# A decoder layer on one core: how the first loads are cut and queued, and the number of warm-up products

## The chip, the core and the metric

The kernel runs on one core of a Trainium2 chip. A core has five engines that run side by side and wait for one another on semaphores: TensorE (PE, matrix products into PSUM), VectorE (DVE), ScalarE (ACT), GpSimd (POOL) and SyncE (SP), which here only issues transfers. Transfers from HBM into SBUF (DMA) run on 16 DMA engines; an instruction on an engine's queue starts each of them. The metric is the device time of one execution in microseconds, the median over several runs.

## The reference

One layer of a hybrid decoder, 256 tokens, width 2048, all in float32:

```python
h = rms_norm(x, attn_norm_g[l])
proj = h @ w_in[l]                                   # 2048 x 4096
q, k, v, p = jnp.split(proj, [1024, 2048, 3072], axis=-1)
a = moba_attention(rms_norm(heads(q)), rms_norm(heads(k)), heads(v), rel_bias)   # 8 heads of 128
m = multiscale_pool(p, pool_w[l], pool_scale[l])     # causal windows 2, 4, 8, 16
x = x + jnp.concatenate([a, m], axis=-1) @ w_out[l]
x = x + conv_ffn(rms_norm(x, ffn_norm_g[l]), w_up[l], conv_w[l], conv_b[l], w_down[l])
```

(The norms' gains are left out in the line of `a`.) The feed-forward part has 2 x 5632 columns up, a causal depthwise convolution of width 3, a SiLU gate and a product down. Nearly all the time is the five matrix products with `w_in`, `pool_w`, `w_out`, `w_up` and `w_down`.

## The kernel before

**Tiling.** The host lays the weights out as chunks of 128 x 2048 floats (1 MB) in the order in which they are used; a chunk `c` holds two units, `u = 2c` and `2c + 1`, of 128 x 1024. A float32 product is made of three products of two-part numbers: each weight unit is split into `wh` (rounded, written by ScalarE, L111) and `wl` (the rest, by VectorE, L112), and each activation tile likewise into its two parts (`x_split`, L174 and L175, for the first product). TensorE multiplies `wh` with both parts and `wl` with the first.

**The first stage.** The program begins with the value columns of `w_in`, in steps of `tok_half` (L125 to L134). One step uses one unit: two k-tiles of 512 columns, and for each k-tile six products of 128 x 512 (four with `wh`, two with `wl`), all at L132. So unit 0 needs the k-tiles 0 and 1 of x and the first half of chunk 0, unit 2 the k-tiles 4 and 5 of x and the first half of chunk 1, and so on; eight units make a block.

**The order of work.** There is no planner: the order of instructions on each engine is the order in which this program writes them. Before the first step it writes all first loads, then `x_split(k)` and `split_piece` for the eight k-tiles 0 to 7, alternating, 512 columns at a time, so that ScalarE makes xh 0, wh 0, xh 1, wh 1, ... and VectorE the rests in the same order. Unit 4 is split next, as a whole. Then step `u` splits unit `u + 5` (`AHEAD`) and multiplies unit `u`.

**The loads.** Raw chunks live in four buffers (`RAWS`). `load(c, pieces, j)` (L98) transfers piece `j` of `pieces` of a chunk, `load_xT(k0, k1)` (L166) the k-tiles `k0` to `k1` of the transposed x, a k-tile being 128 x 256 floats (128 KB; the first has 8 KB more with the norm's gains). x and the chunks 0 to 3 make 2 + 4 MB and are the first loads. When a chunk is split, `release` (L119) starts the load of the chunk four further on, on SyncE's queue, where it waits for the VectorE instruction that last read the buffer. Transfers of SyncE and ScalarE take eight completion semaphores in turn: in the listing of the program the ninth transfer waits on its queue until the first has landed, the tenth until the second has, and so on.

**The warm-up.** While the first loads are under way TensorE multiplies a tile of ones with itself (L184), into a PSUM tile that nothing reads.

Of the kernel before, what the change touches and what calls it, by code (L numbers as in the profile page):

```python
# [69 lines left out]
def layer(ctx: ExitStack, tc: tile.TileContext, xT, wts, par, relT, ident_d, onehot_d, icnt_d, out):  # L70
    nc = tc.nc
# [15 lines left out]
    def small(name):  # L87
        return sm.tile([P, 512], F32, name=name, tag="small")
# [6 lines left out]

    raws, wparts = {}, {}

    def load(c, pieces=1, j=0, queue=None):  # L98

        if c not in raws:  # L100
            raws[c] = wpool.tile([P, CH], F32, name="raw", tag="raw", bufs=RAWS)
        s = slice(j * CH // pieces, (j + 1) * CH // pieces)
        (queue or nc.sync).dma_start(raws[c][:, s], wts[c][:, s])

    def split_piece(u, lo, n):
        r, o = raws[u // 2], (u % 2) * HALF
# [12 lines left out]
    def release(c):  # L119

        raws.pop(c)
        if c + RAWS < wts.shape[0]:
            load(c + RAWS)
# [42 lines left out]
    def load_xT(k0, k1):  # L166

        c = slice(KT + k0 * S if k0 else 0, KT + k1 * S)
        nc.sync.dma_start(xboth[:, c], xT[:, c])
# [8 lines left out]


    nc.vector.memset(ones, 1.0)  # L180
    load(0, 4, 0, nc.scalar)
    ps = small("ps_start")
    for _ in range(7):
        nc.tensor.matmul(ps[:, :P], ones, ones, start=True, stop=True)  # L184
    nc.scalar.preload_act_table_set("natural_log_exp_and_others")

    for k in range(4):
        load_xT(k, k + 1)
        if k:
            load(0, 4, k)  # L190
    for u in range(2, 8):
        load_xT(2 * u, 2 * u + 2)
        load(u // 2, 2, u % 2)
    for k in range(8):
        x_split(k, k + 1)
        split_piece(k // 2, (k % 2) * 512, 512)
# [276 lines left out]
    for b in range(2):  # L473
# [4 lines left out]
        for j in range(4):  # L478
            h, u = 4 * b + j, at + 2 * j
# [198 lines left out]
```

## Time and profile before

| | us |
|---|---|
| median of 3 runs | 1048.32 (1047.69 to 1049.33) |
| profiled execution | 1049.49 |
| its span, first instruction to last | 1047.70 |
| TensorE busy | 1039.4 |
| VectorE busy | 715.8 |
| ScalarE busy | 537.4 |

The profiled execution is one run of the program with the hardware profiler; its own time is a little longer than its span. In the views, L111 is line 111 of the kernel; "out<-in" names the tiles an instruction writes and reads; "[1.14 <-ACT wh L111]" says that the engine stood idle for 1.14 us and what ended the idle time. An engine's queue is marked with a q (SPq, ACTq): these rows are instructions that issue a transfer. Matrix products are pipelined, so a row's busy time overlaps that of the next; the pace of TensorE is read from the starts.

### The profile page before, as it was taken

To read this page: it belongs to the slowest core of one execution; us is meant where nothing else is said; L and a number is where in the kernel's file an instruction comes from. 1 tells how busy PE (TensorE), PEld (TensorE's weight loads), DVE (VectorE), ACT (ScalarE), POOL (GpSimd) and SP (SyncE) were. 2 spreads that over 40 slices of the span, in tenths; PEclk is the share of its full clock that TensorE was granted. 3 is DMA by queue.
4 is the path that set the end of the run, shared out by engine and by line. 5 is a ranking of instruction groups with operands and counts; after the bars stand their busy time and mean duration, and the time that the engine had idled before them with its cause. 6 is when DMAs were issued, how large, how long until landed. Compare 5 with 4: busy or idle time off the path is not lost.

```text
span 1047.7 us, 14301 instructions
## 1 busy us (share of the span) xinstructions
PE 1039.4 (99%) x5784; PEld 898.9 (86%) x5784; DVE 715.8 (68%) x906; ACT 537.4 (51%) x709; POOL 54.8 (5%) x44
## 2 busy tenths in 40 slices
PE   9999999999999999999999999999999999999998
PEld 7878788888888888888888888888888888888887
DVE  6845657776667777777555677777765567777762
ACT  7644544555645555565444455555544445555541
POOL 0500003600110000000000000000000000000000
PEclk9999999999999999999999999999999999999999
DMA  9777554556454445445555445455465545445541
GB/s 348 264 213 226 186 181 141 181 218 225 163 202 176 184 173 220 171 165 219 206 188 188 161 170 220 174 186 216 161 224 179 199 154 210 161 182 219 211 152 41
DMA packets 31395, 200.47 MB, mean 191 GB/s; under 512 B 3816, under 2 KB 4872, under 8 KB 8544
## 3 DMA queue, kind: packets, MB, share of 16 engines
q1 hardware_dynamic: 30192, 196.66, 51.1%
q0 software_dynamic: 992, 2.63, 1.5%
q8 instruction: 45, 0.74, 0.3%
q10 hardware_dynamic: 144, 0.26, 0.1%
q14 instruction: 22, 0.18, 0.1%
HBM read 195.86 MB, written 3.67 MB: 190 GB/s over the span
## 4 chain that ended last, share of the span: by engine, by line
PE 94%; DMA 2%; DVE 2%; POOL 1%; ACT 1%; issue 0%; ACTq 0%; DVEq 0%; POOLq 0%
PE ps_feat L139 54%; PE ps_feat L141 27%; PE ps_tok L132 10%; DMA raw<-in_wts 2%; PE ps_feat L148 1%; DVE wl L112 1%; PE ps_pool L148 1%; PE ps_s L321 1%; POOL pa L380 0%; DMA xboth<-in_xT 0%; ACT wh L111 0%; PE ps_T L308 0%; PE ps_av L353 0%; PE ps_eT L343 0%; DVE m L292 0%
## 5 line engine op out<-in xcount | busy, mean ns | idle before, releaser
L112 DVE TENSOR_TENSOR wl<-raw,wh 128x1024 fp32r<-128x1024 f32 (+1 forms) x366 | 445.0, 1251 | 180.8 <-ACT wh L111 180.1
L139 PE MATMUL ps_feat<-x2h,wh 128*128 128x512 f32 x1408 | 493.2, 393 | 0.0
L111 ACT ACTIVATE wh<-raw 128x1024 fp32r<-128x1024 f32 (+1 forms) x366 | 368.8, 1041 | 136.0 <-PE ps_feat L139 96.5
L141 PE MATMUL ps_feat<-x2h,wl 128*128 128x256 f32 x1408 | 392.8, 279 | 0.0
L139 PEld LDWEIGHTS ps_feat<-x2h,wh 128*128 128x128 f32 x1408 | 263.8, 187 | 62.9
L141 PEld LDWEIGHTS ps_feat<-x2h,wl 128*128 128x128 f32 x1408 | 263.8, 187 | 0.0
L139 PE MATMUL ps_feat<-hid,wh 128*128 128x512 f32 x680 | 238.1, 393 | 0.0
L141 PE MATMUL ps_feat<-hid,wl 128*128 128x256 f32 x680 | 189.7, 279 | 0.0
L139 PEld LDWEIGHTS ps_feat<-hid,wh 128*128 128x128 f32 x680 | 127.4, 187 | 30.3
L141 PEld LDWEIGHTS ps_feat<-hid,wl 128*128 128x128 f32 x680 | 127.4, 187 | 0.0
L369 ACT ACTIVATE fs<-ps_feat 128x512 f32<-128x512 f32 x75 | 44.9, 599 | 129.9 <-PE ps_feat L141 129.9
L132 PE MATMUL ps_tok<-wh,xh 128*128 128x512 f32 x384 | 108.3, 404 | 1.1 <-ACT wh L111 1.1
L370 DVE TENSOR_TENSOR fs<-ps_feat,fs 128x512 f32<-128x512 f32 x75 | 51.9, 692 | 63.9 <-ACT fs L369 63.9
L139 PE MATMUL ps_feat<-cat,wh 128*128 128x512 f32 x256 | 89.7, 393 | 0.0
L132 PEld LDWEIGHTS ps_tok<-wh,xh 128*128 128x128 f32 x384 | 72.4, 191 | 18.7 <-ACT wh L111 1.4
L556 ACT ACTIVATE y<-u,pv 128x256 f32<-128x256 f32 x88 | 48.2, 595 | 65.8 <-DVE u L551 65.8
L141 PE MATMUL ps_feat<-cat,wl 128*128 128x256 f32 x256 | 71.4, 279 | 0.0
L557 DVE SCALAR_TENSOR_TENSOR y<-u,pv,y 128x256 f32<-128x256 f32 x88 | 42.3, 481 | 29.7 <-ACT y L556 29.7
L132 PE MATMUL ps_tok<-wl,xh 128*128 128x512 f32 x192 | 60.9, 399 | 0.0
L139 PEld LDWEIGHTS ps_feat<-cat,wh 128*128 128x128 f32 x256 | 48.0, 187 | 11.3
L141 PEld LDWEIGHTS ps_feat<-cat,wl 128*128 128x128 f32 x256 | 48.0, 187 | 0.0
L139 PE MATMUL ps_feat<-xh,wh 128*128 128x512 f32 x128 | 46.6, 404 | 0.0
(112 smaller groups left out, 555.6 us busy)
## 6 DMA issues: line engine op xcount, KB each, us to landing
raw<-in_wts SPq DMA_DIRECT2D x177, 1024.0 KB, 4.9
raw<-in_wts SPq DMA_DIRECT2D x6, 512.0 KB, 7.8
x<-in_xT SPq DMA_DIRECT2D x1, 2048.0 KB, 9.3
out<-x SPq DMA_DIRECT2D x7, 256.0 KB, 2.0
xboth<-in_xT SPq DMA_DIRECT2D x6, 256.0 KB, 7.6
band<-rsb POOLq DMA_DIRECT2D x1, 1536.0 KB, 37.3
T<-band POOLq DMA_DIRECT2D x2, 512.0 KB, 7.5
raw<-in_wts SPq DMA_DIRECT2D x3, 256.0 KB, 4.1
```

The lines of the kernel that those rows point to most:

```text
L111: nc.scalar.activation(wh, w, AF.Copy)
L112: nc.vector.tensor_tensor(wl, w, wh.bitcast(F32), op=OP.subtract)
L132: nc.tensor.matmul(ps[:, t, :], act[:, k0 + k, a, t * P:(t + 1) * P], w[:, ws], start=(first and k == 0 and n == 0), stop=(last and k == 1 ...
L139: nc.tensor.matmul(ps, wh[:, ws], act[:, k, :, :], start=(first and n == 0), stop=False, skip_group_check=True)
L141: nc.tensor.matmul(ps[:, S:], wl[:, ws], act[:, k, 0, :], start=False, stop=(last and n == len(ks) - 1), skip_group_check=True)
L148: nc.tensor.matmul(ps, w[:, ws], act[:, k, a, :], start=(first and n == 0 and i == 0), stop=(last and n == len(ks) - 1 and i == 2))
L321: nc.tensor.matmul(ps[:, s], qT[:, j, t * P:(t + 1) * P], kT[:, j, :(t + 1) * P], start=(t == 0), stop=True, skip_group_check=True)
L369: nc.scalar.activation(dst, ps[:, :, S:], AF.Copy)
L370: nc.vector.tensor_tensor(dst, ps[:, :, :S], dst, op=OP.add)
L556: nc.scalar.activation(y[:, m, :], u[:, m, 2:], AF.Identity, scale=cw[2], bias=col(C_CB + f))
L557: nc.vector.scalar_tensor_tensor(y[:, m, :], u[:, m, 1:1 + S], cw[1], y[:, m, :], op0=OP.mult, op1=OP.add)
```

## The change

The first piece of chunk 0 is no longer issued from ScalarE's queue. All first loads stand in SyncE's queue, x and weights by turns: k-tile 0 and 1 of x each with a quarter of chunk 0, then k-tiles 2 and 3 with the second half of chunk 0, then four k-tiles with a whole chunk, three times. There were 20 first loads, 19 of them on SyncE, and there are 12. Nine warm-up products stand where seven stood. The splits, the products and all later loads are written in the same order as before.

```diff
-    def load(c, pieces=1, j=0, queue=None):
+    def load(c, pieces=1, j=0):
...
-        (queue or nc.sync).dma_start(raws[c][:, s], wts[c][:, s])
+        nc.sync.dma_start(raws[c][:, s], wts[c][:, s])
...
     nc.vector.memset(ones, 1.0)
-    load(0, 4, 0, nc.scalar)
     ps = small("ps_start")
-    for _ in range(7):
+    for _ in range(9):
         nc.tensor.matmul(ps[:, :P], ones, ones, start=True, stop=True)
     nc.scalar.preload_act_table_set("natural_log_exp_and_others")
 
-    for k in range(4):
-        load_xT(k, k + 1)
-        if k:
-            load(0, 4, k)
-    for u in range(2, 8):
-        load_xT(2 * u, 2 * u + 2)
-        load(u // 2, 2, u % 2)
+    for k0, k1 in ((0, 1), (1, 2), (2, 4)):
+        load_xT(k0, k1)
+        load(0, 4 // (k1 - k0), k0 // (k1 - k0))
+    for c in range(1, 4):
+        load_xT(4 * c, 4 * c + 4)
+        load(c)
     for k in range(8):
         x_split(k, k + 1)
         split_piece(k // 2, (k % 2) * 512, 512)
```

## The prediction

> **What bounds the kernel now.** I read the busy table first, then the chain of waits for the first 45 us, the timeline of the first 14 us, and the DMA issues of that stretch with their times to landing.
>
> ```profile
> PE 1039.4 (99%) x5784; PEld 898.9 (86%) x5784; DVE 715.8 (68%) x906; ACT 537.4 (51%) x709; POOL 54.8 (5%) x44
> ...
> PEclk9999999999999999999999999999999999999999
> ```
>
> TensorE is busy for all but 8.3 of 1047.7 us. The chain of the first 45 us (start, length, what):
>
> ```profile
> 0.74 3.71 DMA xboth<-in_xT
> 4.47 0.51 ACT xh L174
> 4.98 0.53 ACT wh L111
> 5.55 38.26 PE ps_tok L132 x156
> ```
>
> The end hangs on the first x piece, ScalarE's two copies (xh, wh) and the first product at 5.55; from there TensorE never waits until 43.81. A change of the first loads can therefore act only by moving products before about 20 us. Such a shift then reaches the end whole, because the later loads are tied to the splits, not to the clock (SP's waits over the whole run: us, times, longest):
>
> ```profile
> SPq L103 <- DVE wl L112: 897.2, 175, 10.5
> ```
>
> The timeline, merged (start, length, engine; "x4" counts instructions):
>
> ```profile
> 0.74 0.41 ACTq L103 DMA_DIRECT2D raw<-in_wts  x1
> 0.74 0.86 SPq L169 DMA_DIRECT2D xboth<-in_xT  x2
> 1.06 3.35 PE L184 MATMUL ps_start<-ones 128*128 128x128 f32 x14 [1.06 <-DVE ones L180]
> 1.65 0.42 SPq L103 DMA_DIRECT2D raw<-in_wts  x1
> 3.58 0.43 SPq L103 DMA_DIRECT2D raw<-in_wts  x1
> 4.89 0.61 ACT L111 ACTIVATE wh<-raw 128x512 fp32r<-128x512 f32 x1
> 5.03 0.43 SPq L103 DMA_DIRECT2D raw<-in_wts  x1
> 5.55 2.08 PE L132 MATMUL ps_tok<-wh,xh 128*128 128x512 f32 x4 [1.14 <-ACT wh L111]
> 5.99 0.43 SPq L103 DMA_DIRECT2D raw<-in_wts  x1
> 8.28 1.33 PE L132 MATMUL ps_tok<-wh,xh 128*128 128x512 f32 x4
> 9.91 1.10 PE L132 MATMUL ps_tok<-wh,xh 128*128 128x512 f32 x4
> 11.19 0.63 ACT L111 ACTIVATE wh<-raw 128x512 fp32r<-128x512 f32 x1 [2.26 <-DMA raw<-in_wts]
> 11.32 1.10 PE L132 MATMUL ps_tok<-wh,xh 128*128 128x512 f32 x4
> 12.13 0.62 ACT L111 ACTIVATE wh<-raw 128x512 fp32r<-128x512 f32 x1
> 12.73 1.10 PE L132 MATMUL ps_tok<-wh,xh 128*128 128x512 f32 x4
> 13.14 1.05 SPq L103 DMA_DIRECT2D raw<-in_wts  x2
> 13.86 0.69 DVE L112 TENSOR_TENSOR wl<-raw,wh 128x512 fp32r<-128x512 f32 x1
> ```
>
> A k-tile is six products. From 9.91 to 11.32 and on to 12.73 it takes 1.41 us; the first took 2.73 (5.55 to 8.28) and the second 1.63. So 1.32 + 0.22 = 1.54 us were lost to slow first products, though the granted clock in the page's slices reads 90% or more from the first on. The second thing to see is 11.19: ScalarE had idled 2.26 us for the first half of chunk 1, and that wh was ready at 11.82, only 0.91 us ahead of the product at 12.73 that reads it. This is the nearest miss in the stretch.
>
> **The loads.** Issues with KB and us to landing, asked for the stretches around 1.65, 3.58, 5.03, 5.99 and 13.14 us:
>
> ```profile
> raw<-in_wts SPq DMA_DIRECT2D x1, 256.0 KB, 4.0
> raw<-in_wts SPq DMA_DIRECT2D x1, 256.0 KB, 4.2
> raw<-in_wts SPq DMA_DIRECT2D x1, 512.0 KB, 6.1
> raw<-in_wts SPq DMA_DIRECT2D x1, 512.0 KB, 7.1
> raw<-in_wts SPq DMA_DIRECT2D x1, 512.0 KB, 7.8
> ```
>
> Counting the pieces issued up to each, 1544 KB (136 + 3*128 + 4*256) had landed at 3.58+4.2 = 7.8 us; 2312 KB at 11.1; 3080 KB, which ends chunk 1, at 5.99+7.1 = 13.1; 6152 KB, which ends chunk 3, at 13.14+7.8 = 20.9. The engines were never short of work; they were slow in one stretch (busy times, then granted clock, DMA share, GB/s):
>
> ```profile
> 8.00:12.50 4.50, 4.50 (x20) 3.59 (x19) 2.25 (x6) 2.23 (x5) 0.00 (x0) 1.00 0.98 320
> 13.00:18.00 5.00, 5.00 (x23) 4.04 (x22) 4.85 (x9) 5.00 (x10) 0.00 (x0) 1.00 1.04 413
> ```
>
> **The change, part by part.**
>
> *Chunk 0's first piece goes from ACT's queue to the second place of SP's.* ACT is rid of a 0.41 us issue, worth nothing: its next wait is for x at 4.47. The weights are issued at about 1.2 instead of 0.74 (two SP issues took 0.86). With the 4.0 us of the piece issued at 1.65 they land at 5.2, wh takes 0.61, and the first product starts near 5.85: +0.3. The lower bound is 0, since x alone held ScalarE to 4.47 and SP's queue now has less beside it. I take +0.3.
>
> *Two more warm-up products.* Seven end at 4.41, so one is 3.35/7 = 0.48 us, and nine end near 5.4, ahead of 5.85: they delay nothing. What they can bring is at most the 1.54 us, if TensorE is at full rate from its first product. Then unit 2 (chunk 1's first half) is wanted at 5.85 + 4*1.41 = 11.5; without it, at 13.0. Both ends stay open, and the next part decides whether they matter.
>
> *Fewer, larger pieces: 20 loads become 12.* SP issues seven fewer (7*0.43 = 3 us of its queue) and is past all of them by about 6.5 us. Chunks 4 and 5, next in that queue, go out earlier but stand behind the first loads, so they gain and cost nothing. Chunk 0's second half is now one piece; 1544 KB still end it, so by the row above it lands near 7.8, its wh is ready at 8.4, and TensorE wants it at 5.85 + 2.82 = 8.7: covered by 0.3 us. Chunk 1 is the part without cover. It was two halves with x between, wh waiting for 2312 KB; it is now a single 1024 KB piece behind four x tiles, and ScalarE's wait for it ends only when 3080 KB have landed. The trace of before bounds that: 13.1, when the same bytes had landed, from above; from below, 7.8 plus 1536 KB at the steady rate of (6152-3080)/(20.9-13.1) = 394 KB/us = 3.9 us, so 11.7. I take 12.7, an estimate near the upper end: 13.1 is the row of the same bytes in the same stretch, and the slowness there (320 against 413 GB/s) has no cause that the trace names, so most of it is kept; 0.4 us of the 1.4 between the ends is credited to fewer and longer transfers. wh then takes 0.62 and TensorE about 0.04, so unit 2 starts at 13.4 instead of 12.73: **+0.65 us**. The warm-up's gain and the first product's loss both lie in front of this wait and are swallowed by it: unit 2 is wanted at 11.5 to 13.0 in either case. Were the cover gone (an early chunk 1), they would be worth -1.54 and +0.3.
>
> *Behind it.* In the trace of before ScalarE went on from one k-tile's wh to the next in 0.94 us (11.19, 12.13) against 1.41 on TensorE, so each later wh gains about 0.47 us; DVE runs a step behind (the row at 13.86 is the wl of unit 3's first k-tile, which TensorE reaches at 12.73 + 2.82 = 15.55). Chunk 2 ends at 4616 KB, by the steady rate at 13.1 + 3.9 = 17.0, chunk 3 at 20.9; units 4 and 6, their first readers on TensorE, come at 13.4 + 5.64 = 19.0 and 24.7. No second wait.
>
> *Sum.* Profiled execution: 1049.49 us, 1.79 outside the span. It stands 1.17 above the median of 1048.32. Part of that is the slow first products: unit 2 cannot start before the 11.82 of its wh, 0.91 earlier than profiled, and I give the fastest run (1047.69) that start; the other 1.80 - 0.91 = 0.89 I put down to profiling. So 1049.49 + 0.65 - 0.89 = **1049.25 us**, +0.9 on the median. The new kernel should also scatter less, since the wait for chunk 1 no longer depends on how fast the first products run.
>
> The Trainium skill's page "DMA: Bandwidth & Descriptors", section "Anatomy of one DMA", fits a transfer as about 2.0 us plus its bytes at 436 GB/s. As an estimate by that page, 3080 KB from 0.74 would have landed near 10.0, and chunk 1 would make TensorE wait for nothing. The trace does not agree: those bytes had landed at 13.1.
>
> **The rivals.**
>
> *B, chunk 1 arrives in time (faster side).* If the slow stretch of 8 to 12.5 us does not come back, it lands at 11.7, unit 2 starts at 12.37, and the time is 1049.25 - 1.03 = 1048.2. For it: from 13 us on the same queue moved 413 GB/s. Against it: nothing in the change touches the cause, as far as one is to be seen. Earlier still, with TensorE at full rate, 11.5 is the floor: 1047.35. To be faster by more than 0.2% (2.1 us, about what a measurement of this kernel can tell from no change, so under 1046.2) about 1.1 us of the 1.79 outside the span would have to go with ACT's unused queue too; no row shows such a cost. Call that D.
>
> *C, chunk 1 arrives as late as the next whole chunks do (slower).* The first two 1024 KB pieces, issued at 13.86 and 15.57:
>
> ```profile
> raw<-in_wts SPq DMA_DIRECT2D x1, 1024.0 KB, 9.5
> raw<-in_wts SPq DMA_DIRECT2D x1, 1024.0 KB, 11.0
> 15.57 0.33 SPq L103 DMA_DIRECT2D raw<-in_wts  x1
> ```
>
> Issued near 4.0, chunk 1 would by these land at 13.5 to 15.0; the middle, 14.25, gives unit 2 at 14.9 and 1050.75. From a landing of about 13.9 on it is slower by more than 0.2%. Against it: the first of them had up to 4096 KB to wait for, itself included (7176 less the 3080 landed at 13.1), chunk 1 has 3080.
>
> *G, the wait slows TensorE again (slower).* If the full rate comes early, TensorE stands from 11.5 to 13.4, 1.9 us, longer than any pause after its start. If that costs the slow rate once more, the price is again about 1.54 us: 1050.8. No row of before shows such a pause.
>
> The page "TensorE: Matmul & The Clock Gate" of the Trainium skill, Part 1, has the array at half clock until a window of some 3.4 us, running freely, was busy, and back there after about as long an idle one. The doubled first k-tile (2.73 against 1.41) agrees with its first half; by its second, 1.9 us would not suffice, and G would be empty.
>
> That the nine products change nothing of the rate is no separate case: the forecast does not need them.
>
> **How the numbers follow.** Forecast 0.48 (its own range 1048.8 to 1050.1, landing 12.2 to 13.5), B 0.18, C 0.18, G 0.10, D 0.06. The range runs from B to the middle of C and a little past: 1047.8 to 1051.2, leaving out D and the later half of C. Slower by over 0.2% (above 1050.4): C, G and 0.02 of the forecast, 0.30. Faster: D, 0.06. Within: 0.64.
>
> **What would show it.** In the new profile: ScalarE's wait before the first wh of chunk 1 ends at 12 to 13.5 us and TensorE has a gap there of 0.4 to 2 us (right), or no gap (B), or one past 14 (C); first k-tile at 1.4 instead of 2.73 us shows the warm-up worked; k-tiles of over 2 us after the gap show G. If the first product starts after 6.5 us, the first step was mis-sized; if a gap stands at chunk 0's second half or at chunk 2, the cover that I claim there was wrong.

## The result and the profile after

The changed kernel takes 1050.77 us (median of 15 runs, 1050.05 to 1051.83); the kernel before, over 15 runs, 1049.18 (1047.69 to 1050.01). The ratio is 1.0015, with an interval of 1.0008 to 1.0021: about 1.6 us slower, inside the 0.2% that the prediction took as its bound, though the interval just reaches past it. The profiled execution of the changed kernel took 1050.82 us, its span 1049.0. The busy table says as little as before:

```profile
PE 1040.2 (99%) x5788; PEld 899.0 (86%) x5788; DVE 715.9 (68%) x906; ACT 537.7 (51%) x709; POOL 54.6 (5%) x44
```

TensorE's busy time has grown by 0.8 us, about what the two added products take (4.21 us for nine, 3.35 for seven), and its idle time by 0.5. Where the time went is read from the chain of waits of the first 45 us (start, length, what):

```profile
2.59 0.43 SPq L169
...
3.06 0.43 SPq L103
...
3.54 0.43 SPq L169
...
4.01 9.55 DMA raw<-in_wts
...
13.58 0.64 ACT wh L111
...
14.26 30.95 PE ps_tok L132 x131
```

The chain no longer runs over x and the first product at 5.55. It runs through SyncE's queue (rows like the first three, back to 0.74) to the issue of chunk 1 at 4.01, waits 9.55 us for it to land, and only then goes on over ScalarE to unit 2 on TensorE at 14.26. The timeline of the changed kernel, cut to the rows that answer to those of before:

```profile
1.06 4.21 PE L183 MATMUL ps_start<-ones 128*128 128x128 f32 x18 [1.06 <-DVE ones L180]
...
2.91 0.51 ACT L174 ACTIVATE xh<-xboth 128x256 fp32r<-128x256 f32 x1 [0.90 <-DMA xboth<-in_xT]
...
4.62 0.63 ACT L111 ACTIVATE wh<-raw 128x512 fp32r<-128x512 f32 x1 [1.20 <-DMA raw<-in_wts]
...
5.30 2.02 PE L132 MATMUL ps_tok<-wh,xh 128*128 128x512 f32 x4
...
7.62 1.10 PE L132 MATMUL ps_tok<-wh,xh 128*128 128x512 f32 x4
...
9.08 0.63 ACT L111 ACTIVATE wh<-raw 128x512 fp32r<-128x512 f32 x1 [1.22 <-DMA raw<-in_wts]
...
9.77 1.20 PE L132 MATMUL ps_tok<-wh,xh 128*128 128x512 f32 x4 [0.58 <-ACT wh L111]
...
13.58 0.63 ACT L111 ACTIVATE wh<-raw 128x512 fp32r<-128x512 f32 x1 [2.15 <-DMA raw<-in_wts]
...
14.26 1.20 PE L132 MATMUL ps_tok<-wh,xh 128*128 128x512 f32 x4 [1.42 <-ACT wh L111]
...
15.77 1.10 PE L132 MATMUL ps_tok<-wh,xh 128*128 128x512 f32 x4
```

Four things changed on the way to unit 2. The first product starts at 5.30 instead of 5.55 (-0.25). The first two k-tiles end at 7.62 + 1.41 = 9.03, so they lost 0.91 us to slow products instead of 1.54 (-0.63). Unit 1 waits from 9.03 to 9.77 for chunk 0's second half (+0.74). Unit 2 could start at 9.77 + 2.82 = 12.59 and starts at 14.26 (+1.67). The sum is +1.53, which is 14.26 - 12.73. The two whole executions differ by 1.33, because some 0.2 us come back later: a wait of TensorE for the query heads (ps_T) is 0.3 us in place of 0.7.

The rate of the DMA engines in three stretches (busy times, then granted clock, DMA share, GB/s), first before, then after:

```profile
4.50:8.00 3.50, 2.45 (x6) 1.99 (x7) 2.95 (x6) 3.45 (x8) 0.00 (x0) 1.00 1.05 377
8.00:12.50 4.50, 4.50 (x20) 3.59 (x19) 2.25 (x6) 2.23 (x5) 0.00 (x0) 1.00 0.98 320
12.50:18.00 5.50, 5.50 (x25) 4.45 (x24) 5.35 (x11) 5.50 (x11) 0.00 (x0) 1.00 1.03 408
```

```profile
4.50:8.00 3.50, 3.47 (x12) 2.67 (x12) 1.86 (x4) 2.17 (x4) 0.00 (x0) 1.00 0.91 274
8.00:12.50 4.50, 3.92 (x18) 2.79 (x16) 2.56 (x5) 2.06 (x4) 0.00 (x0) 1.00 1.01 395
12.50:18.00 5.50, 4.08 (x18) 3.06 (x17) 3.76 (x8) 4.42 (x10) 0.00 (x0) 1.00 1.03 429
```

The slow stretch did not stay at 8 to 12.5 us; it moved to 4.5 to 8. Over both stretches together the engines moved nearly the same: 377 x 3.5 + 320 x 4.5 = 2760 thousand bytes before, 274 x 3.5 + 395 x 4.5 = 2737 thousand after.

### The profile page after: what moved, and what is told of

It is laid out like the page before. It is cut to its first block, busy times and chain, and to the rows that moved or that the text cites. A ratio compares the mean times of both kernels' runs of the same rounds, so it can differ in the third digit from the quotient of the medians.

```text
span 1049.0 us, 14294 instructions
## 1 busy us (share of the span) xinstructions
PE 1040.2 (99%) x5788; PEld 899.0 (86%) x5788; DVE 715.9 (68%) x906; ACT 537.7 (51%) x709; POOL 54.6 (5%) x44
## 3 DMA queue, kind: packets, MB, share of 16 engines
HBM read 195.86 MB, written 3.67 MB: 190 GB/s over the span
## 4 chain that ended last, share of the span: by engine, by line
PE 94%; DMA 2%; DVE 2%; POOL 1%; ACT 1%; issue 0%; SPq 0%; ACTq 0%; DVEq 0%; POOLq 0%
PE ps_feat L139 54%; PE ps_feat L141 27%; PE ps_tok L132 10%; DMA raw<-in_wts 2%; PE ps_feat L148 1%; DVE wl L112 1%; PE ps_pool L148 1%; PE ps_s L319 0%; POOL pa L378 0%; ACT wh L111 0%; PE ps_T L306 0%; PE ps_av L351 0%; PE ps_eT L341 0%; DVE m L290 0%; POOL pst L380 0%
```

## The experiments

Theory W, from the prediction: a product waits for all bytes up to the end of its piece, the wait for chunk 1 sets the time, and what happens ahead of it is swallowed. Its rivals are given with each run. Times are medians; each kernel ran beside the kernel before. Starts and landings are read from the one profiled execution of each kernel.

**Seven products again.**

```diff
 # the changed kernel
-    for _ in range(9):
+    for _ in range(7):
```

> The changed kernel with seven warm-up products again, nothing else. Theory W (the wait for the whole chunk 1 swallows what the warm-up does): unit 2 still starts at 14.0 to 14.5 us, because the wait for chunk 1 ends at about 13.5; the median stays within 0.3 us of the changed kernel's 1050.77. Rival (the two products carry a gain of their own that reaches the end): slow first products cost up to 0.6 us more, and the median is 0.6 to 1.3 us above, 1051.4 to 1052.1.

Measured: 1051.01 us (1050.22 to 1051.81), 0.24 above the changed kernel. In its profile:

```profile
5.25 2.08 PE L132 MATMUL ps_tok<-wh,xh 128*128 128x512 f32 x4 [0.84 <-ACT wh L111]
...
7.98 1.53 PE L132 MATMUL ps_tok<-wh,xh 128*128 128x512 f32 x4
...
10.56 1.20 PE L132 MATMUL ps_tok<-wh,xh 128*128 128x512 f32 x4 [0.58 <-ACT wh L111]
...
14.33 1.19 PE L132 MATMUL ps_tok<-wh,xh 128*128 128x512 f32 x4 [0.70 <-ACT wh L111]
```

The first k-tile takes 2.73 us again and unit 1 is 0.79 us later (10.56 against 9.77), yet unit 2 is only 0.07 later. The wait in front of unit 2 swallowed the difference, as theory W has it.

**Nine products with the old loads.**

```diff
 # the kernel before
-    for _ in range(7):
+    for _ in range(9):
```

> The kernel before with nine warm-up products, loads as they were. Theory W: with the old loads nothing waits behind the first products until about 11.8 us, so a faster start reaches the end: median 0.3 to 1.2 us under the kernel before (1049.18 over 15 runs), 1048.0 to 1048.9, and the slow runs near 1049.9 become rare. Rival (the two products do nothing for the rate): 1049.0 to 1049.4 with the same scatter. The second look at the old loads also shows whether the slow stretch of the DMA engines from 8 to 12.5 us comes back at the same place: if it belongs to these loads, about 320 GB/s there again; if it is chance, elsewhere or nowhere.

Measured: 1048.43 us (ten runs 1047.98 to 1049.06, one 1050.21), 0.75 under the 1049.18 of the runs beside it, but a ratio of 0.9998 with an interval of 0.9989 to 1.0006, which alone settles nothing (the quarters below do). The profile shows the mechanism: the first k-tile takes 1.50 us (5.38 to 6.88) and unit 2 starts at 11.61, after a wait of 0.35 us.

```profile
5.38 1.20 PE L132 MATMUL ps_tok<-wh,xh 128*128 128x512 f32 x4
...
6.88 1.10 PE L132 MATMUL ps_tok<-wh,xh 128*128 128x512 f32 x4
...
11.61 1.20 PE L132 MATMUL ps_tok<-wh,xh 128*128 128x512 f32 x4 [0.35 <-ACT wh L111]
```

The slow stretch is at its old place, 317 GB/s from 8 to 12.5 us and 366 from 4.5 to 8, so with the same loads it came back once.

**Chunk 1 in halves again.**

```diff
 # the changed kernel
-    for c in range(1, 4):
+    for u in range(2, 4):
+        load_xT(2 * u, 2 * u + 2)
+        load(u // 2, 2, u % 2)
+    for c in range(2, 4):
         load_xT(4 * c, 4 * c + 4)
         load(c)
```

> The changed kernel with chunk 1 in two halves again and the k-tiles 4 to 7 of x in two pairs, ordered as before; chunks 2 and 3 whole, first piece on SyncE's queue, nine products. Theory W (a product waits for all bytes up to the end of its piece): the first half of chunk 1 now ends at 2312 KB instead of 3080, at about 13.5 - 768/390 = 11.6 us, unit 2 starts at 12.6 where the products before it end, and the median falls by 1.3 to 1.7 us to 1049.1 to 1049.5. Rival (the loads as a whole are slow in the new order, and the size of chunk 1's piece does not matter): unit 2 stays near 14.2 and the median within 0.3 us of 1050.77.

Measured: 1049.70 us, 1.07 under the changed kernel; ten of its eleven runs are faster than the fastest of the changed kernel's fifteen (1050.05). Unit 2 starts at 12.45, 1.81 us earlier than in the changed kernel, which is theory W. That the time fell by less has a reason the theory left out. TensorE now reaches unit 4 at 18.08, while chunk 2, still one piece, is not split:

```profile
17.61 0.63 PE L132 MATMUL ps_tok<-wl,xh 128*128 128x512 f32 x2
18.34 1.20 PE L132 MATMUL ps_tok<-wh,xh 128*128 128x512 f32 x4
19.60 0.73 PE L132 MATMUL ps_tok<-wl,xh 128*128 128x512 f32 x2
20.17 1.10 PE L132 MATMUL ps_tok<-wh,xh 128*128 128x512 f32 x4
```

Unit 4 starts 0.26 us late and its first k-tile takes 1.83 instead of 1.41 us, because the wl of a whole unit follows its wh: 0.7 us in all.

**The first piece on ScalarE's queue again.**

```diff
 # the changed kernel, load() with its queue argument as before the change
+    load(0, 4, 0, nc.scalar)
...
-        load(0, 4 // (k1 - k0), k0 // (k1 - k0))
+        if k0:
+            load(0, 4 // (k1 - k0), k0 // (k1 - k0))
```

> The changed kernel with chunk 0's first piece on ScalarE's queue again. Theory W: the first product moves by under 0.3 us and the wait for chunk 1 swallows it; median within 0.3 us of 1050.77. Rival (two queues draw more from the DMA engines in the first 8 us than one does, and the changed kernel lost its time there): chunk 0's second half lands near 7.8 instead of 9.1, chunk 1 near 12.5 instead of 13.55, and the median is about 1 us lower, 1049.8.

Measured: 1050.26 us, 0.51 under the changed kernel: between the two expectations, and the runs of the two kernels overlap. The DMA engines moved 297 GB/s from 3 to 4.5 us (264 in the changed kernel, but only 270 in the kernel before, which has the piece on ScalarE's queue too), ScalarE took up chunk 0's second half at 9.06 (9.08 there) and chunk 1 at 13.41 instead of 13.58. If two queues draw more at first, little of it reaches chunk 1.

**Holding the later loads back.** In each, x from k-tile 8 and chunks 2 and 3 wait behind a small store of a split result, into a tile that nothing reads.

```diff
 # the changed kernel; likewise in the kernel before with nine products,
 # there after k == 2, with a column of unit 1's wl and the chunks in halves
-    for c in range(1, 4):
-        load_xT(4 * c, 4 * c + 4)
-        load(c)
+    load_xT(4, 8)
+    load(1)
...
         x_split(k, k + 1)
         split_piece(k // 2, (k % 2) * 512, 512)
+        if k == 1:
+            nc.sync.dma_start(gate_d, wparts[0][1][:, 1023:1024].bitcast(F32))
+            for c in range(2, 4):
+                load_xT(4 * c, 4 * c + 4)
+                load(c)
```

> The changed kernel, with the k-tiles 8 to 15 of x and the chunks 2 and 3 held back on SyncE's queue behind a 512-byte store of the last column of the rest of k-tile 1, so that they are issued from about 8 us on instead of 4.5 to 7.2. The first eight loads are as in the changed kernel. Theory Q (transfers that stand queued behind slow those in front, so the 220 GB/s from 4.5 to 6 us come from the deep queue): over 330 GB/s from 4.5 to 8 us, chunk 0's second half landed by 8.0 instead of 9.06, chunk 1 by 12.2 instead of 13.55, median 1049.2 to 1049.8. Rival P (the rate belongs to the pieces being moved, whatever stands behind): 220 to 300 GB/s again, chunk 1 at 13.3 to 13.8, median 1050.5 to 1051.0.

> The kernel before with nine products and the k-tiles 8 to 15 of x and the chunks 2 and 3 (in halves, as before) held back on SyncE's queue behind a 512-byte store of part of the rest of k-tile 2, so that they are issued from about 8 us on instead of 6.3. Theory Q: the slow stretch of 8 to 12.5 us (320 GB/s in the kernel before, about 300 and 332 in the second look) goes, chunk 1's first half lands by 10.4 instead of 10.9 to 11.1 and unit 2 starts at 11.0 to 11.3 with fast first products; median 1047.9 to 1048.3. Rival P: the slow stretch stays, median within 0.3 us of 1048.43, or above it if the held-back loads make unit 4 wait.

Measured: 1056.85 and 1054.55 us. Both kernels are far slower than theory Q or an unchanged rate gave, for a reason that had nothing to do with the question (below). The question itself can be read only from the time before the store was issued, at 7.91 and 8.46 us. In the changed kernel with its later loads held back:

```profile
4.50:8.00 3.50, 2.80 (x13) 1.87 (x12) 1.90 (x4) 2.18 (x4) 0.00 (x0) 1.00 0.87 263
8.00:12.50 4.50, 3.12 (x14) 2.22 (x13) 2.38 (x5) 2.07 (x4) 0.00 (x0) 1.00 1.02 392
12.50:18.00 5.50, 4.20 (x19) 3.09 (x17) 3.40 (x7) 3.40 (x7) 0.00 (x0) 1.00 1.24 159
```

With nothing queued behind the first eight loads the rate from 4.5 to 8 us is 263 GB/s, in the changed kernel 274. For the new order theory Q, the deep queue, falls. For the old order the run says less: its held-back loads were in the queue again from 8.83 us on, so that its 311 GB/s from 8 to 12.5 us (317 without the hold) is no rate without a queue behind. While nothing stood behind, from 6.3 to 8.8 us, it moved 331 GB/s, and 361 without the hold: no gain there either.

**Chunk 0 in four pieces too.**

```diff
 # the changed kernel with chunk 1 in halves
-    for k0, k1 in ((0, 1), (1, 2), (2, 4)):
+    for k0, k1 in ((0, 1), (1, 2), (2, 3), (3, 4)):
```

> The changed kernel with chunk 0 in four pieces, one k-tile of x before each, and chunk 1 in halves, as before the change; all on SyncE's queue, chunks 2 and 3 whole, nine products. It differs from the kernel with only chunk 1 in halves by chunk 0's second half. Theory W (a product waits for the bytes up to the end of its piece): the gap ahead of unit 1, 0.9 us there, falls under 0.3, unit 2 starts 0.4 to 0.9 us earlier than its 12.45, and the median is 1048.8 to 1049.4 against 1049.7. Rival (the gap came from the slow first 7 us, not from the piece): the gap stays above 0.5 us and the median within 0.3 of 1049.7.

Measured: 1049.74 us, the same as with chunk 1 alone in halves. The wait at unit 1 is all but gone (unit 1 at 8.48 instead of 9.54), but unit 2 starts at 12.31 instead of 12.45, because chunk 1's first half lands no earlier (this profile, at 1050.29, is the slowest of the eleven runs), and unit 4 waits the longer for chunk 2 (at 18.98, 0.95 us late, and again with a longer first k-tile). Theory W's number was missed since it stopped at one wait; the wait moved to the next piece. The rival's number came, but not by the rival's path: it had kept the gap at unit 1.

**Chunks 2 and 3 whole, alone.**

```diff
 # the kernel before with nine products
-    for u in range(2, 8):
+    for u in range(2, 4):
         load_xT(2 * u, 2 * u + 2)
         load(u // 2, 2, u % 2)
+    for c in range(2, 4):
+        load_xT(4 * c, 4 * c + 4)
+        load(c)
```

> The kernel before with nine products and only the chunks 2 and 3 whole, with four k-tiles of x each: the part of the change that lies behind the tight loads, done alone. Theory Q (what stands behind slows what stands in front): chunk 1's first half lands later than the 10.9 us of the kernel before with nine products, by 0.5 to 1 us, and the median is 0.3 to 0.8 above its 1048.43. Theory W alone (only the bytes up to a piece's end count): chunk 1 as early as there; chunk 2 as one piece ends at 4616 KB, near 16.5 us, and may cost unit 4 up to 0.5 us; median 1048.4 to 1048.9.

Measured: 1048.93 us, 0.50 above the kernel with nine products and the old loads. The median fits theory Q and stands at the edge of theory W, so the landing has to decide. Chunk 1's first half came no later (taken up at 10.61 against 10.93), so theory Q has no support here either; unit 4 started at 17.76, 0.74 us late. That is theory W at the next chunk. Against the kernel with chunk 0 in four pieces this one differs by the first piece's queue and the order of the first four loads, and that is 0.81 us (1048.93 against 1049.74): chunk 1's first half is taken up at 10.61 instead of 11.63 (first this kernel, then the one with chunk 0 in four pieces).

```profile
10.61 0.63 ACT L111 ACTIVATE wh<-raw 128x512 fp32r<-128x512 f32 x1 [1.12 <-DMA raw<-in_wts]
```

```profile
11.63 0.63 ACT L111 ACTIVATE wh<-raw 128x512 fp32r<-128x512 f32 x1 [1.49 <-DMA raw<-in_wts]
```

So the move to one queue has a price after all where the wait behind it is short.

**Chunk 1 whole, alone.**

```diff
 # the kernel before
-    for u in range(2, 8):
+    load_xT(4, 8)
+    load(1)
+    for u in range(4, 8):
         load_xT(2 * u, 2 * u + 2)
         load(u // 2, 2, u % 2)
```

> The kernel before with one part of the change alone: chunk 1 as one piece behind the k-tiles 4 to 7 of x. Seven products, first piece on ScalarE's queue, chunks 2 and 3 in halves. Theory W: ScalarE's wait for chunk 1 ends near the 13.1 us at which the same bytes had landed in the profile of before, unit 2 starts at 13.8 instead of 12.73 (or 11.8 in a run with fast first products), and the median is 1.0 to 1.5 us above the kernel before. Rival (the loss belongs to the queue, the order and the pieces together, none of them alone): within 0.4 us of the kernel before.

Measured: 1050.27 us against 1049.10 beside it, a ratio of 1.0015 (1.0006 to 1.0024). This one part gives most of the change's loss.

```profile
13.51 1.20 PE L132 MATMUL ps_tok<-wh,xh 128*128 128x512 f32 x4 [2.18 <-ACT wh L111]
14.55 0.63 PE L132 MATMUL ps_tok<-wl,xh 128*128 128x512 f32 x2
15.02 1.10 PE L132 MATMUL ps_tok<-wh,xh 128*128 128x512 f32 x4
```

Chunk 1 landed at 12.8 and unit 2 started at 13.51. TensorE stood 2.18 us ahead of it, and the k-tile behind the pause took 1.51 us: no slow rate followed this pause.

**Chunk 1's first half in quarters.**

```diff
 # the kernel before with nine products
-    for u in range(2, 8):
+    for k in range(4, 6):
+        load_xT(k, k + 1)
+        load(1, 4, k - 4)
+    for u in range(3, 8):
         load_xT(2 * u, 2 * u + 2)
         load(u // 2, 2, u % 2)
```

> The kernel before with nine products and the first half of chunk 1 in two quarters, each behind one k-tile of x: finer where the change is coarser. Theory W: the bytes ahead of unit 2 fall from 2312 to 1928 KB, at the 300 GB/s of that stretch over 1 us earlier, so unit 2 no longer waits (0.35 us in the kernel before with nine products) and starts at 11.0 to 11.3; median 1048.0 to 1048.4, at or under the 1048.43 there. Rival (two more transfers cost SyncE's queue and the semaphores more than they bring): 1048.6 to 1049.2.

Measured: 1047.92 us (1047.32 to 1048.25), a ratio of 0.9987 with an interval of 0.9978 to 0.9996 to the kernel before: this version beats both. In its profile every k-tile from the first on follows without a wait:

```profile
5.49 1.21 PE L132 MATMUL ps_tok<-wh,xh 128*128 128x512 f32 x4 [0.22 <-ACT wh L111]
...
6.99 1.10 PE L132 MATMUL ps_tok<-wh,xh 128*128 128x512 f32 x4
...
8.40 1.10 PE L132 MATMUL ps_tok<-wh,xh 128*128 128x512 f32 x4
...
9.81 1.10 PE L132 MATMUL ps_tok<-wh,xh 128*128 128x512 f32 x4
...
11.21 1.10 PE L132 MATMUL ps_tok<-wh,xh 128*128 128x512 f32 x4
```

**The same with seven products.**

```diff
 # the kernel with quarters
-    for _ in range(9):
+    for _ in range(7):
```

> The fastest kernel so far (nine products, first half of chunk 1 in quarters, median 1047.92) with seven products again. Theory W: with no wait ahead of unit 2, every slow first product reaches the end, so the scatter of the kernel before comes back: runs between 1047.3 and 1049.6, median 1048.4 to 1049.0. Rival (the quarters alone made the gain, the two products nothing): median within 0.2 us of 1047.92 and the same narrow scatter of 0.9 us.

Measured: 1049.11 us (1047.49 to 1049.59), just above theory W's range and 1.19 above the one with nine (the two did not run side by side), and no longer faster than the kernel before (ratio 1.0001, 0.9992 to 1.0010). In its profile the first k-tile takes 2.73 us and the second 2.25, and unit 2 starts at 13.00. The rival falls: where nothing waits behind the first products, the two added ones are worth about a microsecond. What they do is to make the fast rate more likely: three of the eleven runs with seven products lie under 1048.2, eight above 1048.8; of the eleven with nine, all lie under 1048.3.

**x on the second queue.**

```diff
 # the kernel before with nine products; k-tiles 0 to 3 of x on ScalarE's queue, chunk 0 on SyncE's
 # (load_xT takes a queue)
-    load(0, 4, 0, nc.scalar)
+    for k in range(4):
+        load_xT(k, k + 1, nc.scalar)
...
     for k in range(4):
-        load_xT(k, k + 1)
-        if k:
-            load(0, 4, k)
+        load(0, 4, k)
```

> The kernel before with nine products, the k-tiles 0 to 3 of x on ScalarE's queue and all of chunk 0 on SyncE's: the opposite of the change's single queue. Theory T (two queues draw more from the DMA engines in the first 5 us than one): from 3 to 4.5 us at least the 307 to 331 GB/s seen with one piece on ScalarE's queue, against 229 to 255 with SyncE alone; chunk 1's first half by 10.5, no wait ahead of unit 2, median 1047.9 to 1048.4. Rival (only what stands ahead counts, whichever queue carries it): 240 to 300 GB/s, and the first product later than 5.4 us, because x shares the engines with more weights; median 1048.5 to 1049.0.

Measured: 1050.06 us. Theory T falls in this form: from 3 to 4.5 us the engines moved 177 GB/s, below the rival's range too. The rival's late first product came, and later than it gave: x landed at 5.4, the first product started at 6.54 and unit 2 at 14.31. That x comes late because it shares the engines with more weights fits this, but why the rate is so low is not shown. Part of unit 2's delay is the slow rate of TensorE, which came in this profile in spite of nine products (its 1050.73 us is the slowest of the eleven runs):

```profile
6.54 2.08 PE L132 MATMUL ps_tok<-wh,xh 128*128 128x512 f32 x4 [1.28 <-ACT wh L111]
...
9.27 1.45 PE L132 MATMUL ps_tok<-wh,xh 128*128 128x512 f32 x4
...
11.02 1.10 PE L132 MATMUL ps_tok<-wh,xh 128*128 128x512 f32 x4
```

The first two k-tiles took 2.73 and 1.75 us, 1.66 more than two of 1.41.

**All runs on one scale.** If the first stage is the whole story, the profiled time less unit 2's start is the same in every kernel.

| kernel | unit 2 starts | profiled time | difference |
|---|---|---|---|
| nine products, quarters | 11.21 | 1047.53 | 1036.3 |
| nine products, old loads | 11.61 | 1048.38 | 1036.8 |
| before | 12.73 | 1049.49 | 1036.8 |
| seven products, quarters | 13.00 | 1049.30 | 1036.3 |
| before, chunk 1 whole | 13.51 | 1050.33 | 1036.8 |
| changed, first piece on ScalarE's queue | 14.10 | 1050.61 | 1036.5 |
| changed | 14.26 | 1050.82 | 1036.6 |
| x on ScalarE's queue | 14.31 | 1050.73 | 1036.4 |
| changed, seven products | 14.33 | 1050.86 | 1036.5 |

The differences stay within 0.5 us while unit 2 moves by 3.1. The three kernels that have chunk 2 in one piece and unit 2 before 12.5 stand 1037.3 to 1038.0 above it, by the late unit 4. The two kernels with the store are left out: they lose most of their time at unit 4 (below).

## Why the prediction was right, and where its steps were not

The measured time lies in the range, and the ratio's interval lies mostly within the 0.2% that was given the largest chance. The place and the mechanism were as forecast: the chain runs through chunk 1, the one part without cover; ScalarE's wait for it ends at 13.55, just past the forecast's 12 to 13.5 us and at the lower end of rival C's 13.5 to 15.0; and the warm-up is swallowed there. But 1050.77 is outside the forecast's own range of 1048.8 to 1050.1, and two things here are luck. C's 1050.75 is met only because two errors cancel: unit 2 starts 0.64 us earlier than C's 14.9, and C carries the 0.89 us that the sum below should not have taken off. And the time is above the 1050.4 at which the prediction let "slower by over 0.2%" begin; the difference is below 0.2% only because the median of the kernel before rose from 1048.32 over 3 runs to 1049.18 over 15. Step by step:

- *First product near 5.85.* It started at 5.30. The issue is later by 0.44 us as said, but x and the piece landed sooner than the rows of before gave (us to landing, issued at 0.74 and 1.18):

```profile
xboth<-in_xT SPq DMA_DIRECT2D x1, 136.0 KB, 2.1
raw<-in_wts SPq DMA_DIRECT2D x1, 256.0 KB, 3.4
```

  Before, x took 3.7 us with the weights beside it on the other queue, and it takes 3.7 again in the run with the first piece back on ScalarE's queue. The step's price was +0.3, measured -0.25; behind the wait for chunk 1 neither counts.
- *The two products delay nothing, and are swallowed.* Right: they end at 5.27, and with seven the median is 0.24 us higher, which is within the scatter. The sign that was named for the warm-up, a first k-tile of 1.4 us, did not show: it took 2.32 (5.30 to 7.62). What they would be worth without the cover was put at up to 1.54; the medians of the two kernels with quarters differ by 1.19.
- *Chunk 0's second half is covered by 0.3 us.* Wrong: it landed at 9.06 instead of 7.8 and unit 1 waited 0.74 us. The step took the landing of the same bytes from before, where the DMA engines were fast from 4.5 to 8 us, and in the new order they are slow just there. It cost nothing in the end, since unit 2 waited for chunk 1 behind it; with chunk 1 in halves, too, chunk 0 in four pieces gave the same time.
- *Chunk 1 lands at 12.7, at most 13.1.* It landed at 13.55, and this term, +0.65 forecast and +1.53 measured for unit 2's start, is the one mis-sized. It landed 9.5 us after its issue, the figure of the first of the two whole chunks that C went by, so it stands as near to C's lower end as to the forecast's upper:

```profile
raw<-in_wts SPq DMA_DIRECT2D x1, 1024.0 KB, 9.5
```

  The upper bound was none, and not for want of bytes moved: by 13.1 us the DMA engines had moved 3.66 MB before and 3.67 MB after. But before, the 3080 KB (3.15 MB) up to the end of chunk 1 had landed by then, and after only at 13.55, with 3.90 MB moved: 0.75 MB beyond those bytes, against 0.51 before. The step counted only the bytes in front of a landing. Whether pieces behind chunk 1 went ahead of its last bytes, and why more of them than before, no run shows. (The prediction's other figure, 10.0, comes from a fit that the Trainium skill's page "DMA: Bandwidth & Descriptors" gives for one transfer issued by GpSimd; here SyncE issues a dozen, so the miss tells nothing of that fit.)
- *No second wait.* Right for the changed kernel, though only because unit 2 is late: where chunk 1 came earlier, the whole chunk 2 cost 0.7 us or more at unit 4.
- *The sum.* Against the profile of before, 0.65 was forecast and 1.33 measured, 0.68 too little. The 0.89 us that was "put down to profiling" was a second error. The 1047.69 of the table is not a floor from which the others rise by profiling: over 15 runs before lies between 1047.69 and 1050.01, and the profiled 1049.49 is an ordinary one among them. 0.68 + 0.89 - 0.05 (the median after is 0.05 under its profile) is the whole miss of 1.52.
- *Less scatter.* Weakly so: the 15 runs span 1.78 us in place of 2.32.
- *The rivals.* B did not come: the slow stretch moved ahead instead of going away. G did not come: behind pauses of 1.42 and 2.18 us the next k-tile took 1.51. Its mechanism exists, though, for longer pauses: in the two kernels with the store TensorE stood for 4.02 and 5.41 us ahead of unit 4, and the next k-tile took 2.57 us (24.52 to 27.09) and 2.73 us (23.55 to 26.28). The first of them, the kernel after the change with the store:

```profile
24.52 1.93 PE L132 MATMUL ps_tok<-wh,xh 128*128 128x512 f32 x4 [4.02 <-ACT wh L111]
26.24 1.05 PE L132 MATMUL ps_tok<-wl,xh 128*128 128x512 f32 x2
27.09 1.57 PE L132 MATMUL ps_tok<-wh,xh 128*128 128x512 f32 x4
```

  By the page "TensorE: Matmul & The Clock Gate" of the Trainium skill, Part 1, a pause shorter than about 3.4 us keeps the full rate; all four pauses agree. D was not seen.

How the 1.6 us are made up can be read from a chain of medians, each kernel one part away from the one before it (not all taken side by side: the kernel before itself moved between 1048.68 and 1049.18 from one set of runs to another, and the interval of each ratio to it is some 0.9 us to either side). The table shows sizes; the -0.75 and the +0.50 would not stand by their medians alone, and rest on the profiles above:

| step | us | difference |
|---|---|---|
| before | 1049.18 | |
| nine products | 1048.43 | -0.75 |
| chunks 2 and 3 whole | 1048.93 | +0.50 |
| first piece on SyncE's queue | 1049.74 | +0.81 |
| chunk 0's second half whole | 1049.70 | -0.04 |
| chunk 1 whole: the changed kernel | 1050.77 | +1.07 |

## What to carry to other kernels

A larger piece is not free at the start of a kernel: its first reader waits for its last byte, and the piece to look at is the one whose reader has the least slack, here chunk 1, not the first piece. Cut finer exactly there, and a warm-up that was worth next to nothing behind a wait can be worth its price, about a microsecond here. A landing time taken from the old order is no bound for a new one; the slow stretch can move with the pieces.

## What the runs showed of the hardware that was not expected

While a store of 512 bytes, 4 from each of 128 partitions, was under way, the DMA engines were slow for more than 5 us: in the run above that held the changed kernel's later loads back they moved 159 GB/s from 12.5 to 18 us at a share of 1.24, where the changed kernel moved 429, and the store landed 11.0 us after its issue. Four loads had been issued behind it by then, so work was not lacking. Both kernels with it were 6 to 8 us slower than the kernel before, the slow rate behind the pause at unit 4 included; no run separates the store from the holding back. The Trainium skill's page "DMA: Bandwidth & Descriptors", section "Specifications", says that transfers under 512 B make the engine read, modify and write; the time of these runs goes in that direction, but the traces do not show it apart.

TensorE's slow first rate comes and goes under a granted clock that reads 1.00 in the profiles. With seven products the first four of unit 0 took 2.08 us in three of four profiles and 1.21 in the fourth; with nine they took 1.20 to 1.33 in seven of ten and 1.90 to 2.08 in the other three, one of them behind an idle stretch of 1.28 us. The page "TensorE: Matmul & The Clock Gate" of the Trainium skill, Part 1, has a window that runs freely and so a warm-up that depends on its phase; the scatter of the runs with seven products (2.1 us with the quarters) and its fall to 0.9 with nine fit that, but no run shows the window itself.

Why the DMA engines are slow for a few microseconds, and why that stretch comes at 8 to 12.5 us with the old pieces and at 4.5 to 8 with the new ones, stays open. For the new order the depth of the queue is excluded. Chance is not: two profiles with the loads of before agree (320 and 317 GB/s from 8 to 12.5 us), but of the two with the quarters, whose loads are the same, one has 312 there and the other 372. The size of the pieces in flight and their order remain.
